# Modulation weights: four buffers instead of two, dots one call behind the transfer, another spread of the pieces

## The chip, the cores and the metric

The kernel runs on one core of a Trainium2 chip. The core has five engines with instruction streams of their own: TensorE (PE, matrix products; PEld is its weight load), VectorE (DVE), ScalarE (ACT), GpSimd (POOL) and SyncE (SP), which here issues the transfers from the chip's memory to the core's. Each engine works through its stream in order; semaphores hold an instruction until what it reads is there or what it overwrites is free. The metric is the device time of one execution in microseconds (us).

## The reference

The model has two layers and a width of 1024. Two groups of 256 tokens run through it: the latent tokens (`LAT`) and the context tokens (`CTX`). Each layer is a half FFN, a mixer (attention in layer 0, an mLSTM in layer 1) and a second half FFN; after layer 1's mixer only the latent tokens are needed. Shift, scale and gate of all of these, nine vectors per layer and group, come from a condition vector:

```python
mod_lat = split((silu(c)     @ ada_w[i] + ada_b[i])[:, None, :], 9)
mod_ctx = split((silu(c_ctx) @ ada_w[i] + ada_b[i])[None, None, :], 9)

def half_ffn(h, shift, scale, gate, w_in, w_out, g, b):
    xm = h * (1.0 + scale) + shift
    a, u = split(xm @ w_in, 2)                 # w_in: 1024 x 5632
    y = (silu(a) * u) @ w_out                  # w_out: 2816 x 1024
    return layer_norm(ALPHA * h + 0.5 * gate * y, g, b)
```

`ada_w` is 2 x 1024 x 9216 in float32. All is computed in float32 accuracy.

## The kernel before

Activations lie transposed in the core's memory: 8 tiles of 128 channels by 512 tokens (`h`, in the order listings t_66). A float32 product is made of three matmuls, high times high, high times low and low times high (`mm3`, line 238). For this each weight piece of 128 x 1024 float32 (512 KB, `raw`, the transfer at line 207) is split: ScalarE casts the high part (line 222) and VectorE subtracts it for the low part (line 227). Seven split pairs are kept, so the weights run ahead of PE.

A half FFN runs in two halves of eleven units. An "in" unit `j` multiplies two weight pieces into the gate and the up product; `ffn_g` then does the Silu on ScalarE (line 568), the product with the up part on VectorE (line 569), and splits it into `gh` (a cast, line 222) and `gl` (a subtraction, line 227). After the eleven "in" units come eight "out" units `d`, which each multiply all eleven products by a piece of `ffn_out` and add the result into `h` with the gate (line 692). Two tiles of the residual are also scaled after each "in" unit, by VectorE and ScalarE (lines 543 and 544, `residual`).

The modulation vectors are not computed by PE. `ada_w` comes in pieces of 128 output channels by 1024 (512 KB; `ada_load`, the transfer at line 331, on SP's queue with the other weights), and VectorE takes the dot of a piece with silu(c), and with silu(c_ctx) where that is needed (`ada_dot`, line 337): one instruction per vector. 56 pieces of layer 0 are taken beside the first half FFN, and 72 of layer 1 beside layer 0's second and layer 1's first half FFN. The last 32 pieces of layer 1 have one dot each, all others two. The function `side` makes a callback for each unit, `("in", j)` or `("out", half, d)`, which `ffn` calls after it has written that unit: `pop` in the first half FFN, and `some(n)` in the two others, with `n` from the table `DOTS`, a number of dots. `some` loads a piece and writes its dots behind the load until the number is reached. The buffers of the pieces lie in a pool (`cp`) with the two condition vectors, of which the Silu (line 306) is taken once for each pool; the pool is closed at `SUMSAT`, the fifth "out" unit of the first half (`d == 4`), where the operands of fast products (`fast_operands`, `fast_sums`) take its place, and a new one is opened for the rest.

What sets the order: a scheduler arranges the instructions of each engine, but those that are pinned, the dots, the residual's updates and others, stay in program order on their engine. In front of the norm of each next stage (lines 440 to 522) stands a chain of VectorE and ScalarE work: subtracting the mean (447), squares (454), their sums (464), the reciprocal root, the scaled result in two parts (520 to 522). The mLSTM behind layer 1's first FFN begins with constants (transfer at line 1152, casts at 1154 and 1155, a VectorE sum at 1156, memsets at 1161) and a convolution (1177 to 1181).

Of the kernel before, what the change touches and what calls it, by code (L numbers as in the profile page):

```python
# [18 lines left out]
P = 128  # L19
# [68 lines left out]

SUMSAT = 4
FLIP = 56  # L90
DOTS = {
    1: {("in",): 4, ("out", 0): 3, ("out", 1): 2},
    2: {("in",): 3, ("out", 0): 2, ("out", 1): 3},
}

TAILSTEP = {(0, 3, 1): 'bmccccccc', (1, 0, 2): 'c', (1, 0, 6): 'v', (1, 1, 7): 'rxxxxxxxx'}
# [73 lines left out]
class Body:  # L170
# [98 lines left out]
    def setup(self):  # L269
        nc, a = self.nc, self.a  # L270
        self.cols = col = self.t([P, 3 * BLOCK // 2])
        for i, x in enumerate((1.0, 1.0 / D, 1.0 / (D - P), 0.5 / D)):
            nc.vector.memset(col[:, i : i + 1], x)
        self.mean1, self.half = col[:, 1:2], col[:, 3:4]
        self.ones, self.mean, self.most = (col[:, i : i + 1].broadcast_to([P, P]) for i in range(3))

        self.h = self.t([P, ND, T])
        self.xh = self.t([P, ND, T + BLOCK], F32R)
        self.xl = self.t([P, ND, T + BLOCK], F32R)
        self.ident = self.t([P, P])  # L280
        self.vec = self.t([P, V_N])
        self.mod = {}
        self.s1 = {}

    def silu_c(self):

# [40 lines left out]
    def ada_load(self, layer, dt):  # L327
        if (layer, dt // ND) not in self.mod:
            self.mod[layer, dt // ND] = self.t([P, 2, ND])
        r = self.t([P, 1024], tag="ada", bufs=2, pool=self.cp)  # L330
        self.nc.sync.dma_start(r, self.a["ada_w"][layer, dt])
        return r

# [9 lines left out]
    def ada(self, layer, dt, vecs=(0, 1)):  # L343
        r = self.ada_load(layer, dt)
        for v in vecs:
            self.ada_dot(r, layer, dt, v)

    def modv(self):
        return self.t([P, 2, ND], tag="modv", bufs=12)
# [308 lines left out]
    def ffn(self, layer, s, gate, groups, side, start=None, cpool=None):  # L658
        nc, V = self.nc, self.nc.vector
        li = layer * 2 + s  # L660
        allg = BOTH
        call = lambda *k: side.get(k, lambda: None)()
        with self.tc.tile_pool(name=f"ffn{li}", bufs=1) as gp:
            self.gp, self.gt, self.gw, self.gn = gp, {}, T, NFH
            done = 0
            if start:
                start(self)
                done = NSTART

            def unit_in(j, w, g, steps={}, ks=range(ND), ps=None):  # L670
                n = g[1] - g[0]
                pa, pu = ps or (self.mm(), self.mm())
                for k in ks:
                    for part, o in ((0, pa), (1, pu)):
                        self.mm3(o[:, :n], w(part_k(part, k)), self.x(k, g), k == 0, k == ND - 1)
                    self.steps(steps.get((j, k), ""))
                if ks[-1] < ND - 1:
                    return pa, pu
                self.ffn_g(j, pa, pu, g)

            def unit_out(hf, d, w, g, steps={}):
                t0, t1 = g
                y = self.mm()
                for i in range(NFH):
                    gh, gl = self.gt[hf * NFH + i]
                    self.mm3(y[:, : t1 - t0], w(d * NFH + i), (gh[:, t0:t1], gl[:, t0:t1]), i == 0, i == NFH - 1)
                    self.steps(steps.get((int(g == CTX), d - (ND - TAIL), i), ""))
                for gg in groups:
                    if gg[0] >= t0 and gg[1] <= t1:
                        v = 0 if gg[0] == 0 else 1  # L690
                        z = self.h[:, d, gg[0] : gg[1]]
                        V.scalar_tensor_tensor(z, y[:, gg[0] - t0 : gg[1] - t0], gate()[:, v, d : d + 1], z, ALU.mult, ALU.add)  # L692
                        if hf:
                            self.add_sum(gg, d)

            w_in, w_out = self.a["ffn_in"][li], self.a["ffn_out"][li]
            stream = lambda j: Stream(self, [w_in[2 * j + i] for i in range(2)])
            for hf in range(2):
                js = list(range(hf * NFH, (hf + 1) * NFH))[0 if hf else done :]
                if hf == 0 and not start:  # L700
                    first = js[:LEAD]
                    ws = {j: Keep(self, [w_in[2 * j + i] for i in range(2)], SH) for j in first}
                    assert len(self.running) == 1

                    k0, k1 = range(ND // 2), range(ND // 2, ND)
                    for j in first[:-1]:
                        unit_in(j, ws[j], LAT, LEADSTEP[li])
                    j = first[-1]
                    ps = unit_in(j, ws[j], LAT, ks=k0)
                    assert not self.running  # L710
                    pc = unit_in(first[0], ws[first[0]], CTX, ks=k0)
                    ws[j](ND)
                    unit_in(first[0], ws[first[0]], CTX, ks=k1, ps=pc)
                    unit_in(j, ws[j], LAT, ks=k1, ps=ps)
                    for j in first[1:]:
                        unit_in(j, ws[j], CTX)
                    for j in first:
                        call("in", j)
                    js = js[LEAD:]
                fast = cpool is not None and hf == 1  # L720
                for j in js:
                    if fast:
                        self.fast_in(j, w_in, st)
                        continue
                    unit_in(j, stream(j), allg)
                    assert not self.running
                    if j >= LEAD + FAFTER:
                        self.fine = False
                    call("in", j)
                    self.residual(2, self.pin)  # L730
                if not hf:
                    self.residual(len(self.later))
                w = Stream(self, [w_out[hf * NFH + i] for i in range(NFH)])
                body = ND - TAIL if hf else ND
                if fast:
                    more.close()
                    cpool = self.silu_all()
                for d in range(body):
                    if cpool and not hf and d == SUMSAT:
                        cpool.close()  # L740
                        self.n += 1
                        more = ExitStack()
                        st = more.enter_context(self.tc.tile_pool(name=f"st{self.n}", bufs=1, side="right"))
                        self.fast_operands(st)
                    unit_out(hf, d, w, allg)
                    if cpool and not hf and d >= SUMSAT and d - SUMSAT < 2:
                        self.fast_sums(d - SUMSAT)
                    call("out", hf, d)
                if body < ND:
                    w = Keep(self, w.chunks, SH, w)  # L750
                    self.fine = True
                    for g in groups:
                        for d in range(body, ND):
                            unit_out(hf, d, w, g, TAILSTEP)
                    self.steps('B')
        return cpool
# [823 lines left out]
def emit(ctx, tc, a, out):  # L1580
    b = Body(ctx, tc, a, out)
# [16 lines left out]
    def side(key, coef, keep=(True, True), nxt=True, alone=False, dots={}):  # L1598
        def pop():
            for _ in range(3 if len(queue) > 40 else 2):  # L1600
                if queue:
                    b.ada(*queue.pop(0))

        def some(n):
            while n > 0 and later:
                n -= len(later[0][2])
                b.ada(*later.pop(0))

        get = once(key, coef)

        b.begin = lambda g: b.norm(g, get, keep[0 if g == LAT else 1], nxt, alone)
        s = {}
        for j in range(NF):
            s["in", j] = (lambda: some(dots["in",])) if dots else pop
        for d in range(ND):
            s["out", 0, d] = (lambda d=d: some(dots["out", 0] if d < SUMSAT else 0)) if dots else pop
            s["out", 1, d] = lambda: some(dots.get(("out", 1), 0))
        return s

    both = (LAT, CTX)  # L1620
# [5 lines left out]
    cpool = b.ffn(0, 1, once("g1", lambda: b.half_gate(0, 8)), both, side("n2", lambda: b.ln_mod(0, 2, (1, 0)), dots=DOTS[1]), cpool=cpool)  # L1626
    cpool = b.ffn(1, 0, once("g2", lambda: b.half_gate(1, 2)), both, side("n3", lambda: b.ln_mod(1, 0, (1, 3)), (True, False), dots=DOTS[2]), cpool=cpool)
    assert not later, len(later)
    cpool.close()
    b.mlstm(lambda: b.shift_(1, 5, slice(0, 1)), side("n4", lambda: b.ln_mod(1, 1, (1, 6), 1), alone=True))  # L1630
    b.ffn_last(1, once("g3", lambda: b.half_gate(1, 8, 1)))
# [93 lines left out]
```

## Time and profile before

| | |
|---|---|
| median of 3 runs | 1651.09 us (1650.75 to 1655.48) |
| the profiled execution | 1649.32 us, span 1647.6 us |
| mean granted TensorE clock | 0.993 |
| PE, PEld busy | 1617.8 us, 1457.4 us |
| VectorE busy | 1353.8 us |
| ScalarE busy | 744.2 us |
| GpSimd busy | 61.6 us |
| share of 16 transfer engines, main queue | 47.8% |

The profile is one execution. A row of the timeline gives start and length of a run of like instructions and, in brackets, how long the engine stood idle before it and for what; "t" stands for any unnamed tile. A row of the waits gives the sum, the number and the longest. A window's row gives the length, the busy time of each engine with its count, the granted clock, the share of the transfer engines and their rate. Layer 1's first half FFN has its "in" units from about 970 to 1043 us in this execution, the first "out" units behind them.

### The profile page before, as it was taken

The page shows a single profiled execution, that of the slowest core. Times are in us where ns is not written, and L with a number is a line of the kernel's source. Part 1 is how long each engine was busy: PE and PEld are TensorE (multiplying, and loading weights), DVE is VectorE, ACT ScalarE, POOL GpSimd, SP SyncE. Part 2 cuts the span into 40 slices and gives each one's busy share as a digit, 9 for nine tenths or more (in the row PEclk, how much of TensorE's full clock was granted, in tenths as well). Part 3 has the DMA queues.
Part 4 walks back from the last instruction along what each step waited for, and adds up shares of the span by engine and source line. Part 5 has one row for each costly group of instructions (what it writes and reads, how often), then busy time and mean ns, then how long its engine had stood idle before and what let it go on. Part 6 is the DMA issues. An engine that isn't in the chain of part 4 may idle for free. (4 is left out here: it accounts for less than half of the span.)

```text
span 1647.6 us, 26587 instructions
## 1 busy us (share of the span) xinstructions
PE 1617.8 (98%) x10308; PEld 1457.4 (88%) x10308; DVE 1353.8 (82%) x2689; ACT 744.2 (45%) x1269; POOL 61.6 (4%) x76
## 2 busy tenths in 40 slices
PE   9999999999999999999999999899999999999998
PEld 6888888899988998889999998689999989999987
DVE  5899978649888879999977977799965968897687
ACT  5532222314676343425652433225652656656542
POOL 0000000001011200000000100000000100020000
PEclk9999999999999999999999999899999999999999
DMA  9577765622103247733353267733352342437652
GB/s 371 187 237 231 239 215 187 203 76 84 65 1 91 64 143 229 229 128 129 103 182 126 78 193 255 250 120 116 115 155 66 116 120 78 135 109 256 181 172 96
DMA packets 72495, 252.59 MB, mean 153 GB/s; under 512 B 7984, under 2 KB 10800, under 8 KB 72368
## 3 DMA queue, kind: packets, MB, share of 16 engines
q1 hardware_dynamic: 71792, 250.10, 47.8%
q8 instruction: 81, 1.33, 0.3%
q10 hardware_dynamic: 576, 0.79, 0.1%
q14 instruction: 46, 0.38, 0.1%
HBM read 249.81 MB, written 1.05 MB: 152 GB/s over the span
## 5 line engine op out<-in xcount | busy, mean ns | idle before, releaser
L238 PE MATMUL t<-t,t 128*128 128x256 f32 (+2 forms) x8412 | 1325.1, 319 | 14.2 <-ACT t L222 10.7
L238 PEld LDWEIGHTS t<-t,t 128*128 128x128 f32 x8412 | 1193.1, 189 | 133.9 <-ACT t L222 12.7
L222 ACT CAST t<-t 128x1024 fp32r<-128x1024 f32 (+3 forms) x521 | 429.6, 844 | 467.3 <-PE t L238 244.3
L227 DVE TENSOR_TENSOR t<-t,t 128x256 fp32r<-128x256 f32 (+2 forms) x740 | 514.7, 728 | 116.6 <-ACT t L222 112.5
L337 DVE SCALAR_TENSOR_TENSOR t<-t,t 128x1024 bf16<-128x1024 f32 x224 | 263.5, 1220 | 25.2 <-DMA t<-in_ada_w 24.5
L909 PE MATMUL t<-t,t 128*128 128x256 f32 (+1 forms) x256 | 79.5, 311 | 0.0
L911 PE MATMUL t<-t,t 128*128 128x256 f32 (+1 forms) x256 | 78.8, 308 | 0.0
L910 PE MATMUL t<-t,t 128*128 128x256 f32 (+1 forms) x256 | 78.4, 306 | 0.0
L568 ACT ACTIVATE t<-t 128x512 f32<-128x512 f32 (+1 forms) x71 | 34.3, 487 | 95.6 <-PE t L238 95.6
L692 DVE SCALAR_TENSOR_TENSOR t<-t,t,t 128x256 f32<-128x256 f32 x96 | 42.7, 478 | 37.0 <-PE t L238 37.0
L569 DVE TENSOR_TENSOR t<-t,t 128x512 f32<-128x512 f32 (+1 forms) x71 | 38.9, 551 | 32.8 <-PE t L238 26.7
L464 POOL TENSOR_TENSOR t<-t,t 128x256 f32<-128x256 f32 x30 | 23.4, 781 | 1130.9 <-ACT t L454 1129.7
L1424 PE MATMUL t<-t,t 128*128 128x512 f32 (+3 forms) x286 | 60.2, 365 | 2.0 <-ACT t L1501 1.0
L837 PE MATMUL t<-t,t 128*128 128x512 f32 (+1 forms) x300 | 60.7, 364 | 0.0
L1424 PEld LDWEIGHTS t<-t,t 128*128 128x128 f32 (+2 forms) x286 | 43.8, 159 | 18.3 <-issue 2.2
L837 PEld LDWEIGHTS t<-t,t 128*128 128x128 f32 x300 | 51.4, 189 | 9.1 <-DVE t L831 0.3
L454 ACT ACTIVATE t<-t 128x256 f32<-128x256 f32 x72 | 26.2, 411 | 72.3 <-DVE t L447 72.3
L544 ACT ACTIVATE t<-t,t 128x256 f32<-128x256 f32 x64 | 29.4, 503 | 57.4 <-DVE t L543 57.4
L909 PEld LDWEIGHTS t<-t,t 128*128 128x128 f32 x256 | 48.4, 189 | 2.7
L910 PEld LDWEIGHTS t<-t,t 128*128 128x128 f32 x256 | 48.2, 188 | 2.6
L911 PEld LDWEIGHTS t<-t,t 128*128 128x128 f32 x256 | 48.1, 188 | 2.5
L615 DVE TENSOR_TENSOR t<-t,t 128x512 f32<-128x512 f32 x66 | 45.3, 686 | 1.1 <-DMA t<-in_ffn_in 0.3
(200 smaller groups left out, 1065.5 us busy)
## 6 DMA issues: line engine op xcount, KB each, us to landing
t<-in_ffn_in SPq DMA_DIRECT2D x168, 512.0 KB, 4.1
t<-in_ada_w SPq DMA_DIRECT2D x137, 512.0 KB, 4.2
t<-in_ffn_out SPq DMA_DIRECT2D x66, 512.0 KB, 4.4
t<-in_ffn_last SPq DMA_DIRECT2D x22, 512.0 KB, 3.5
t<-in_att_in SPq DMA_DIRECT2D x12, 512.0 KB, 3.5
t<-in_c SPq DMA_DIRECT2D x8, 512.0 KB, 7.8
t<-in_att_out SPq DMA_DIRECT2D x8, 512.0 KB, 3.5
t<-in_ml_qk SPq DMA_DIRECT2D x8, 512.0 KB, 3.6
```

The costliest lines, as they stand in the source:

```text
L222: self.behind(self.nc.scalar.copy(h, x))
L227: self.behind(self.nc.vector.tensor_tensor(out=ls, in0=xs, in1=hs.bitcast(F32), op=ALU.subtract))
L238: mm = lambda *k, **kw: self.nc.tensor.matmul(*k, skip_group_check=not group, **kw)
L337: ins = nc.vector.scalar_tensor_tensor(self.tmp().bitcast(BF16), r, 1.0, self.cb[:, v, :], ALU.mult, ALU.mult, accum_out=to)
L569: V.tensor_tensor(out=sl, in0=sl, in1=pu[:, :n], op=ALU.mult)
L615: add = lambda o, x, y: V.tensor_tensor(out=o, in0=x, in1=y, op=ALU.add)
L692: V.scalar_tensor_tensor(z, y[:, gg[0] - t0 : gg[1] - t0], gate()[:, v, d : d + 1], z, ALU.mult, ALU.add)
L837: pin(nc.tensor.matmul(o, gs[g], ws[k][w][:, i : i + n], start=k == k0 and g == w == 0, stop=k == k1 - 1 and g == 1,))
L909: mm(o, self.xh[:, k, c], wh, start=k == 0, stop=False)
L910: mm(o, self.xh[:, k, c], wl, start=False, stop=False)
L911: mm(o, self.xl[:, k, c], wh, start=False, stop=k == ND - 1)
L1424: mm = lambda *k, **kw: pin(nc.tensor.matmul(*k, **kw))
```

## The change

Three things change. The pieces get `PIECES = 4` buffers instead of two, in all three FFNs. In the second and third of them `some(n)` first writes the dots of the pieces that the call before has loaded (`flush`), and then loads `n` pieces whose dots are left to the next call; what is left is flushed before a pool is closed. The table `DOTS` now counts pieces, for each unit apart. In layer 0's second half FFN that is 2 pieces after each of the eleven "in" units as before, then 2, 2, 1, 1 (before: 2 each) and 1 each in the second half. In layer 1's first it is 2 pieces after the first four "in" units (before: 2 after three), 3 after the next five and 2 after the last two (before: 3 after all others), 2, 2, 2, 0 in the first four "out" units (before: 2 each), and 2, 2, 2, 1 in the first "out" units of the second half (before: none).

```diff
+PIECES = 4
 DOTS = {
-    1: {("in",): 4, ("out", 0): 3, ("out", 1): 2},
-    2: {("in",): 3, ("out", 0): 2, ("out", 1): 3},
+    1: {**{("in", j): 2 for j in range(11)}, **{("out", 0, d): 2 if d < 2 else 1 for d in range(4)}, **{("out", 1, d): 1 for d in range(4)}},
+    2: {**{("in", j): 2 for j in range(4)}, **{("in", j): 3 if j < 9 else 2 for j in range(4, 11)}, **{("out", 0, d): 2 if d < 3 else 0 for d in range(4)},
+        **{("out", 1, d): 2 if d < 3 else 1 for d in range(4)}},
 }
...
-        r = self.t([P, 1024], tag="ada", bufs=2, pool=self.cp)
+        r = self.t([P, 1024], tag="ada", bufs=PIECES, pool=self.cp)
...
+    def flush(self):
+
+        while self.waiting:
+            r, layer, dt, vecs = self.waiting.pop(0)
+            for v in vecs:
+                self.ada_dot(r, layer, dt, v)
...
                     if cpool and not hf and d == SUMSAT:
+                        self.flush()
                         cpool.close()
...
         def some(n):
-            while n > 0 and later:
-                n -= len(later[0][2])
-                b.ada(*later.pop(0))
+            b.flush()
+            for _ in range(min(n, len(later))):
+                layer, dt, vecs = later.pop(0)
+                b.waiting.append((b.ada_load(layer, dt), layer, dt, vecs))
...
-            s["in", j] = (lambda: some(dots["in",])) if dots else pop
+            s["in", j] = (lambda j=j: some(dots.get(("in", j), 0))) if dots else pop
         for d in range(ND):
-            s["out", 0, d] = (lambda d=d: some(dots["out", 0] if d < SUMSAT else 0)) if dots else pop
-            s["out", 1, d] = lambda: some(dots.get(("out", 1), 0))
+            s["out", 0, d] = (lambda d=d: some(dots.get(("out", 0, d), 0))) if dots else pop
+            s["out", 1, d] = lambda d=d: some(dots.get(("out", 1, d), 0))
...
     assert not later, len(later)
+    b.flush()
     cpool.close()
```

Lines of the changed kernel have numbers 2 to 11 higher (337 becomes 340, 207 becomes 209, 543 and 569 become 553 and 579). A row of the following listings is one instruction with what it writes and reads.

First place: VectorE in layer 1's first half FFN, at the last "in" unit (its product is t_10396 in the listing of before, and t_10376 in that of after; t_10318, t_10322 and t_10326 are pieces that the same call has loaded, t_10222, t_10224 and t_10226 pieces of the call before). Before:

```order
L337 SCALAR_TENSOR_TENSOR t_10320,t_10238<-t_10318,t_8504 128x1024
L337 SCALAR_TENSOR_TENSOR t_10324,t_10238<-t_10322,t_8504 128x1024
L227 TENSOR_TENSOR t_10651<-t_10649,t_10651 128x1024
L337 SCALAR_TENSOR_TENSOR t_10328,t_10238<-t_10326,t_8504 128x1024
L543 SCALAR_TENSOR_TENSOR t_66<-t_66,t_9031,t_9401 128x256 x2
L569 TENSOR_TENSOR t_10396<-t_10396,t_10335 128x512
L227 TENSOR_TENSOR t_10395<-t_10396,t_10394 128x512
L337 SCALAR_TENSOR_TENSOR t_10403,t_10238<-t_10401,t_8504 128x1024
L337 SCALAR_TENSOR_TENSOR t_10407,t_10238<-t_10405,t_8504 128x1024
```

After:

```order
L340 SCALAR_TENSOR_TENSOR t_10299,t_10059<-t_10222,t_8492 128x1024
L340 SCALAR_TENSOR_TENSOR t_10301,t_10059<-t_10224,t_8492 128x1024
L340 SCALAR_TENSOR_TENSOR t_10303,t_10059<-t_10226,t_8492 128x1024
L553 SCALAR_TENSOR_TENSOR t_66<-t_66,t_9014,t_9384 128x256 x2
L229 TENSOR_TENSOR t_10582<-t_10580,t_10582 128x1024
L579 TENSOR_TENSOR t_10376<-t_10376,t_10315 128x512
L229 TENSOR_TENSOR t_10623<-t_10621,t_10623 128x1024
L229 TENSOR_TENSOR t_10375<-t_10376,t_10374 128x512
L340 SCALAR_TENSOR_TENSOR t_10381,t_10059<-t_10305,t_8492 128x1024
L340 SCALAR_TENSOR_TENSOR t_10383,t_10307<-t_10308,t_8492 128x1024
```

Three dots stand ahead of the product in both; in the second the pieces they read were loaded a call earlier, and the subtraction of a weight piece that stood among them is behind the residual's updates.

Second place: SP's queue at the first "in" units of the same FFN. Before:

```order
L207 DMA t_10169<-in_ffn_in 128x1024
L207 DMA t_10198<-in_ffn_in 128x1024
L331 DMA t_9779<-in_ada_w 128x1024
L331 DMA t_9785<-in_ada_w 128x1024
L207 DMA t_10253<-in_ffn_in 128x1024
L331 DMA t_9791<-in_ada_w 128x1024
L331 DMA t_9797<-in_ada_w 128x1024
L207 DMA t_10282<-in_ffn_in 128x1024
L331 DMA t_9804<-in_ada_w 128x1024
L331 DMA t_9808<-in_ada_w 128x1024
```

After:

```order
L209 DMA t_10151<-in_ffn_in 128x1024
L209 DMA t_10180<-in_ffn_in 128x1024
L334 DMA t_9769<-in_ada_w 128x1024
L334 DMA t_9779<-in_ada_w 128x1024
L334 DMA t_9781<-in_ada_w 128x1024
L334 DMA t_9791<-in_ada_w 128x1024
L334 DMA t_9793<-in_ada_w 128x1024
L334 DMA t_9877<-in_ada_w 128x1024
L334 DMA t_9879<-in_ada_w 128x1024
L209 DMA t_10234<-in_ffn_in 128x1024
L334 DMA t_9881<-in_ada_w 128x1024
```

Where transfers of one weight piece and two pieces of `ada_w` took turns, seven pieces of `ada_w` now stand in a row.

Third place: VectorE between the end of that FFN and the context norm of the mLSTM (t_12243, then t_12215, is a sum over channels; t_66 is `h`). Before:

```order
L404 TENSOR_TENSOR t_12243<-t_12243,t_66 128x256
L1156 TENSOR_TENSOR t_12832<-t_69 128x64
L404 TENSOR_TENSOR t_12243<-t_12243,t_66 128x256
L1161 MEMSET t_12838 128x16 x2
L227 TENSOR_TENSOR t_12992<-t_12990,t_12992 128x256 x4
L1179 SCALAR_TENSOR_TENSOR t_12874<-t_12841,t_70,t_12874 128x255
L447 TENSOR_TENSOR t_66<-t_66,t_12891 128x256
L1180 SCALAR_TENSOR_TENSOR t_12874<-t_12841,t_70,t_12874 128x255
L447 TENSOR_TENSOR t_66<-t_66,t_12891 128x256 x3
```

After:

```order
L414 TENSOR_TENSOR t_12215<-t_12215,t_66 128x256
L229 TENSOR_TENSOR t_12992<-t_12990,t_12992 128x256
L414 TENSOR_TENSOR t_12215<-t_12215,t_66 128x256
L340 SCALAR_TENSOR_TENSOR t_12822,t_10555<-t_12374,t_12163 128x1024
L229 TENSOR_TENSOR t_12992<-t_12990,t_12992 128x256
L1167 TENSOR_TENSOR t_12832<-t_69 128x64
L1172 MEMSET t_12838 128x16 x2
L1190 SCALAR_TENSOR_TENSOR t_12874<-t_12841,t_70,t_12874 128x255
L457 TENSOR_TENSOR t_66<-t_66,t_12891 128x256
```

The last dot (line 340) stands behind the last sum, the mLSTM's first instructions behind it, and two of the four subtractions have moved further back.

More of the change, by code (lines that the diff above doesn't have):

```diff
@@ L283, in setup @@
         self.s1 = {}
+        self.waiting = []
     def silu_c(self):
```

## The prediction

> **What bounds the kernel now.** I read the page's busy shares first, then the list of waits, then timelines of one engine each around the longest wait. Durations come from one execution of 1649.32 us, whose span is 1647.6 us; the median of the runs shown, 1651.09 us, is 1.77 us above it. A change of 0.3% (5 us) is about what a measurement of this kernel can tell from none.
>
> ```profile
> span 1647.6 us, 26587 instructions
> ...
> PE 1617.8 (98%) x10308; PEld 1457.4 (88%) x10308; DVE 1353.8 (82%) x2689; ACT 744.2 (45%) x1269; POOL 61.6 (4%) x76
> ...
> L337 DVE SCALAR_TENSOR_TENSOR t<-t,t 128x1024 bf16<-128x1024 f32 x224 | 263.5, 1220 | 25.2 <-DMA t<-in_ada_w 24.5
> ```
>
> The columns of the last row are busy time, mean of one in ns, idle time before them and its cause. PE is busy 98% of the span, so a gain can only come out of the 30 us in which it is not, or out of a slower clock. The dots of the change (L337) cost VectorE 263.5 us, and in front of them it waits 24.5 us for their pieces. VectorE is busy 82%, so that matters only where PE then waits for VectorE. The list of PE's waits, and PE's timeline, show one such place:
>
> ```profile
> PE t L238 <- ACT t L222: 10.7, 4, 7.5
> PE t L1024 <- DVE t L227: 1.7, 2, 1.1
> ...
> 1029.65 20.11 PE L238 MATMUL t<-t,t 128*128 128x512 f32 x88
> 1057.31 22.97 PE L238 MATMUL t<-t,t 128*128 128x512 f32 x89 [7.55 <-ACT t L222]
> ```
>
> (The waits' columns are total, times, longest; the timeline's are start and length in us.) PE stands still for 7.55 us up to 1057.31, in the first half of layer 1's first FFN, where the "in" units have ended and the first "out" unit has begun; it waits for a cast. The next row's longest wait is 1.1 us. PE's windows around it (length, busy and count, granted clock, DMA share, GB/s) price the stall:
>
> ```profile
> 1040.00:1049.00 9.00, 9.00 (x42) 1.00 0.68 228
> 1049.00:1057.00 8.00, 0.76 (x4) 0.70 0.80 268
> 1057.00:1064.00 7.00, 6.69 (x18) 0.62 0.62 213
> 1064.00:1075.00 11.00, 11.00 (x50) 1.00 0.85 260
> ```
>
> From 1064 on, 50 matmuls take 11.00 us, 0.22 us each. The 22 of 1049 to 1064 would take 4.84 us and took 15.00: the stall costs 10.16 us, 2.6 us more than the gap, since the granted clock is 0.62 after it. This is 10.2 us of the whole, and the only sizeable one.
>
> Why the cast is late, backwards: ScalarE, VectorE and the DMA queue, word for word.
>
> ```profile
> 1047.71 0.59 ACT L568 ACTIVATE t<-t 128x512 f32<-128x512 f32 x1
> 1055.65 0.91 ACT L544 ACTIVATE t<-t,t 128x256 f32<-128x256 f32 x2 [7.36 <-DVE t L543]
> 1056.64 1.56 ACT L222 CAST t<-t 128x512 fp32r<-128x512 f32 x2
> ...
> 1049.25 1.22 DVE L337 SCALAR_TENSOR_TENSOR t<-t,t 128x1024 bf16<-128x1024 f32 x1
> ...
> 1050.40 1.22 DVE L227 TENSOR_TENSOR t<-t,t 128x1024 fp32r<-128x1024 f32 x1
> 1053.98 1.23 DVE L337 SCALAR_TENSOR_TENSOR t<-t,t 128x1024 bf16<-128x1024 f32 x1 [2.37 <-DMA t<-in_ada_w]
> ...
> 1055.13 0.88 DVE L543 SCALAR_TENSOR_TENSOR t<-t,t,t 128x256 f32<-128x256 f32 x2
> 1055.93 0.68 DVE L569 TENSOR_TENSOR t<-t,t 128x512 f32<-128x512 f32 x1
> ...
> 1049.36 1.47 SPq L331 DMA_DIRECT2D t<-in_ada_w  x2
> ```
>
> The cast at 1056.64 needs the product L569 of the last "in" unit. Its Silu (L568) was ready at 1048.30, but the product ran at 1055.93, behind three dots and two residual updates (L543). The third dot waited 2.37 us for a piece that could be requested only at 1049.36, when the dot before had freed one of two buffers. This has built up over the whole half: in the stretch of the "in" units, VectorE's waits are
>
> ```profile
> DVE t L337 <- DMA t<-in_ada_w: 14.9, 14, 2.8
> DVE t L227 <- ACT t L222: 6.1, 8, 1.1
> ```
>
> **The change, part by part.**
>
> *Four buffers, dots one call later.* The number of dots ahead of the last unit's product stays the same (I count 33 in both orders, from the first dot of this FFN), so VectorE's work up to there is unchanged. What can go is the 14.9 us of waiting. In the new order a unit of three pieces issues its second and third transfer when the first two dots of the call before have freed buffers, and needs them a call later. Between lies one unit's work on VectorE. The window of one unit length, and the time to landing of these transfers:
>
> ```profile
> 1004.00:1015.00 11.00, 11.00 (x50) 9.09 (x50) 7.95 (x16) 2.92 (x6) 0.00 (x0) 1.00 0.71 242
> ...
> DMA to landing us min/median/max: 3.4/4.2/5.6
> ```
>
> (PE, PEld, DVE, ACT, POOL busy.) VectorE is busy 7.95 us of 11, and a piece lands after 4.2, at worst 5.6 us. 7.95 − 5.6 leaves 2.3 us, so no dot waits, and per unit some 3 us of lag is worked off. Bounds: if all 14.9 us go, the product of the last unit runs as soon as its Silu is there. The product started 1055.93 − 1048.30 = 7.63 us after that Silu, and the Silu itself stood in ScalarE's queue behind residual updates that waited for VectorE as well. PE could go on without it until 1057.31 − 7.55 = 1049.76. So 7.6 us of the 14.9 are enough to close the gap, half of them. Lower bound: none of the waits go, gain 0. Upper bound: the stall is gone, gain 10.2 us. I take the upper end, because it has 7.3 us to spare.
>
> *Other spread of the pieces.* Two pieces instead of three or four dots' worth per unit at the head of this half, 33 pieces instead of 38 before its second half, and 7 instead of none in that second half: 7 × 1.22 = 8.5 us more there for VectorE, where PE doesn't wait for it now. In the FFN before, 32 pieces instead of 34. I cost these at 0; the cover is VectorE's idle time, 18% of the span. If it were gone there, the sums of the fast products would be late next.
>
> *The transfers on SP's queue.* Seven pieces now stand in a row ahead of one piece of in-weights (t_10253, in the new order t_10234), where two did:
>
> ```profile
> 971.82 2.62 SPq L331 DMA_DIRECT2D t<-in_ada_w  x2
> 975.25 0.33 SPq L207 DMA_DIRECT2D t<-in_ffn_in  x1
> ...
> L337 DVE SCALAR_TENSOR_TENSOR t<-t,t x35: 1215/1221/1228, 969.4 to 1059.0; 128x1024 bf16<-128x1024 f32 x35
> ...
> L207 SPq DMA_DIRECT2D t<-in_ffn_out x11: 327/328/328, 999.3 to 1062.2; - x11
> ```
>
> The last of the seven waits for the block of 14 dots, 14 × 1.15 = 16.1 us (1.15 is the distance of 1049.25 and 1050.40) from 969.4, the first dot here, so these weights are asked for at about 985.5 instead of 975.25, 10 us later. Weights run far ahead: the first of "out" is asked for at 999.3 and PE gets to "out" near 1043 (30 matmuls of 0.22 us before 1049.76), 44 us later, of which landing, cast and subtraction take their part. Bounds 0 and a stall of what exceeds that lead; I take 0.
>
> *SiLU of c for layer 1.* With 24 KB the buffer of c no longer fits beside the attention's, so its loads and two activations move from the first FFN's end to the attention's end, where ScalarE is idle:
>
> ```profile
> 323.75 1.06 ACT L306 ACTIVATE t<-t 128x1024 f32<-128x1024 f32 x1 [1.03 <-DMA t<-in_c]
> ...
> 547.77 1.41 ACT L454 ACTIVATE t<-t 128x256 f32<-128x256 f32 x4 [11.32 <-DVE t L447]
> ...
> 576.57 1.28 ACT L568 ACT_TABLE_LOAD   x1
> ...
> DMA to landing us min/median/max: 4.1/7.8/9.5
> ```
>
> Two activations of 1.06 us and a table load of 1.28 us (that of 576.57 moves here with them) are 3.4 us, in a gap of 11.32. Asked for when the gap begins, at 547.77 − 11.32 = 536.45, the buffer lands by these rows at 540.6 to 546, and the activations end at 544 to 549.4. Bounds: 0, and 1.6 us late at the norm whose squares start at 547.77. I take 0, the landing being nearer its minimum where the queue isn't full.
>
> *The last flush.* One dot, 1.15 us, now stands on VectorE between the end of "out" and the context norm of the mLSTM, and tiles of the mLSTM share the memory that closes after it:
>
> ```profile
> 1284.95 0.28 ACT L1155 CAST t<-t 128x128 fp32r<-128x128 f32 x1
> 1285.14 0.40 ACT L1154 CAST t<-t 128x256 fp32r<-128x256 f32 x1
> 1287.09 0.56 ACT L1177 ACTIVATE t<-t,t 128x256 f32<-128x256 f32 x1 [1.55 <-PE t L238]
> 1289.68 0.42 ACT L454 ACTIVATE t<-t 128x256 f32<-128x256 f32 x1 [2.02 <-DVE t L447]
> ...
> 1282.04 0.33 SPq L1152 DMA_DIRECT2D t<-in_const  x1
> ...
> 1287.78 1.09 DVE L227 TENSOR_TENSOR t<-t,t 128x256 fp32r<-128x256 f32 x3
> ...
> 1295.75 1.05 PE L427 MATMUL t<-t,t 128*128 128x1 f32 x8 [0.69 <-DVE t L464]
> ```
>
> PE waits 0.69 us for this norm, so a delay here shows in full. The dot adds 1.15 us; four subtractions (1.09 / 3 = 0.36 each) leave the stretch up to the norm's last sum, 1.45: −0.3 us. The two casts at 1284.95 now wait for the dot, about 3 us, and would still end before the 1289.68 square. If the constants' transfer also waited for the dot (near 1288, 6 us later; it now takes up to 1284.95 − 1282.04 = 2.9 us), the casts would come near 1291 and 1291.5 and hold up the square by about 2 us, with what follows up to 3. Bounds −0.3 and +3; I take 0, since the order lets that transfer go after a norm step that stands ahead of the dot.
>
> *Sum.* 1649.32 − 10.2 + 0 = 1639.1 us for a profiled execution, and 1651.09 − 10.2 = **1640.9 us** as a median: 0.6% faster.
>
> **The rivals.**
>
> *Partly handed back.* The stall goes, but the last flush or the moved SiLU costs 2 to 4 us at its norm. For it: PE's 0.69 us wait there shows no slack. Against it: the working above. 1641 + 3 = 1644 us.
>
> *The stall only shrinks.* VectorE keeps half of its waits or new ones behind ScalarE (the 6.1 us row). With a gap of 3 us left, priced by the stall's own ratio 10.16 / 7.55 = 1.35, 4 us stay: 1645 us; with nothing gained, as the change then does nothing where PE waits, 1651 us. Against it: twice the waiting that must go can go. The Trainium skill (TensorE: Matmul & The Clock Gate, section on the HAM clock gate) says that the clock halves after an idle window of about 3.4 us and comes back after a busy one. The fall to 0.62 after 7.55 us agrees; no row here shows a gap near 3 us. By that rule a 3 us gap would leave the clock alone and cost 3.0, so 1644 us.
>
> *Slower: weights behind waiting pieces.* SP issues in order; a piece that waits for its buffer, which a lagging VectorE frees, holds all weights behind it. The point from which it decides: the weights' lead of 44 us less landing, cast and subtraction (about 15 us), some 29 us. If the pieces were held four more units of 11 us, 44 us, PE would stand 15 us, at 1.35 that is 20: 1651 − 10 + 20 = 1661 us. For it: seven pieces in a row, four buffers that VectorE frees one by one. Against it: I find 10 us of delay, not 29. The Trainium skill (DMA: Bandwidth & Descriptors, Anatomy of one DMA) says that a semaphore wait sits on the issuing sequencer ahead of dispatch, which speaks for this rival; the rows of two pieces in 2.62 and 1.47 us, where one issue takes 0.33, agree.
>
> **How the numbers follow.** Stall gone and little else: 0.60, 1638.5 to 1643. Partly handed back: 0.17, 1643 to 1647. Only shrunk, or unchanged: 0.14, 1644 to 1652. Slower by the weights: 0.09. The predicted time is that of the first, 1641. The range takes in the first two and most of the third: 1637.5 to 1649. Faster by more than 0.3% (below 1646.1): 0.60 + 0.15 + 0.05 = 0.80; within 0.3%: 0.02 + 0.08 + 0.01 = 0.11; slower: 0.09.
>
> **What would show it.** Right: no PE gap above 1.5 us between 1000 and 1100, granted clock 1.00 there, VectorE's waits for pieces down from 24.5 us to under 5, and the last "in" unit's product within 3 us of its Silu. The SiLU of c in ScalarE's gap near 540, with PE's waits up to 580 as short as now; PE's waits from 1275 to 1310 under 3 us in sum. Wrong: a PE gap behind the cast of a product still there, PE waiting for a weight's cast or subtraction in any FFN, or a gap before the norms named. I would be most wrong if VectorE's lag came from the order of the work and not from the waits for pieces.

## The result, and the profile after

| | before | after |
|---|---|---|
| median | 1650.92 us (4 runs, 1649.79 to 1655.48) | 1638.72 us (4 runs, 1638.02 to 1640.61) |
| profiled execution | 1649.32 us, span 1647.6 us | 1640.61 us, span 1638.8 us |
| mean granted clock | 0.993 | 0.999 |

The ratio is 0.9925, with a 95% interval of 0.9907 to 0.9943: the kernel is 0.75% faster, 12.2 us. The forecast was 1641 us with a range of 1637.5 to 1649. A second set of five executions gave 1639.39 us against 1651.36 us, ratio 0.9922 (0.9910 to 0.9934); of the eleven executions of before in it, one of 2002.23 us at a mean granted clock of 0.752 is left out. The profile of before is of an execution 1.6 us under its median, that of after of one 1.9 us above its own.

The page after, the rows that answer to those of before:

```profile
span 1638.8 us, 26592 instructions
...
PE 1616.8 (99%) x10308; PEld 1455.5 (89%) x10308; DVE 1353.5 (83%) x2689; ACT 745.4 (45%) x1269; POOL 62.0 (4%) x76
...
L340 DVE SCALAR_TENSOR_TENSOR t<-t,t 128x1024 bf16<-128x1024 f32 x224 | 260.7, 1219 | 0.0
```

VectorE's 224 dots take what they took, but the idle time in front of them fell from 25.2 us to 0.0. PE's busy time is 1 us less; the span is 8.8 us shorter. PE's waits for the cast fell from 10.7 us (longest 7.5) to 3.1 (longest 1.8). At the turn from "in" to "out" in layer 1's first half FFN, PE's timeline and windows (length, busy and count, granted clock, transfer share, GB/s):

```profile
999.79 110.38 PE L240 MATMUL t<-t,t 128*128 128x512 f32 x518
```

```profile
1040.00:1049.00 9.00, 9.00 (x42) 1.00 0.64 210
1049.00:1057.00 8.00, 8.00 (x37) 1.00 0.93 307
1057.00:1064.00 7.00, 7.00 (x33) 1.00 0.71 216
1064.00:1075.00 11.00, 11.00 (x50) 1.00 0.31 109
```

One run of 518 matmuls without a gap, and 70 matmuls in the 15 us from 1049 to 1064 where 22 stood before, at full clock. VectorE and ScalarE at the last "in" unit:

```profile
1038.79 1.22 DVE L229 TENSOR_TENSOR t<-t,t 128x1024 fp32r<-128x1024 f32 x1
1042.68 0.69 DVE L579 TENSOR_TENSOR t<-t,t 128x512 f32<-128x512 f32 x1 [2.67 <-ACT t L578]
```

```profile
1041.99 0.60 ACT L578 ACTIVATE t<-t 128x512 f32<-128x512 f32 x1 [2.57 <-PE t L240]
1042.61 1.57 ACT L224 CAST t<-t 128x1024 fp32r<-128x1024 f32 x2
```

Before, the product (line 569, now 579) came 7.6 us after its Silu, behind three dots. Now VectorE stands idle for 2.67 us until the Silu is there, and the Silu itself waits for PE and not for VectorE.

Between two marks that both kernels have, PE's first norm matmul of the context group at 910.12 (909.77 after) and the same at 1275.66 (1265.00), the time went from 365.54 to 355.23 us: 10.3 us less in the stretch that holds the stall. The rest of the profiled executions differs by 1.5 us in sum and in both directions: 1.1 us later at the start, 1.5 us earlier through the attention, 0.2 us earlier at the start of the mLSTM, 2.0 us later behind it.

### The profile page after: what moved, and what is told of

Same layout as the page of the kernel before. It is cut to its first block, busy times and chain, and to the rows that moved or that the text cites. A ratio compares the mean times of both kernels' runs of the same rounds, so it can differ in the third digit from the quotient of the medians.

```text
span 1638.8 us, 26592 instructions
## 1 busy us (share of the span) xinstructions
PE 1616.8 (99%) x10308; PEld 1455.5 (89%) x10308; DVE 1353.5 (83%) x2689; ACT 745.4 (45%) x1269; POOL 62.0 (4%) x76
## 5 line engine op out<-in xcount | busy, mean ns | idle before, releaser
L531 ACT ACTIVATE t<-t,t 128x256 fp32r<-128x256 f32 x72 | 32.8, 503 | 27.4 <-DVE t L530 27.4
```

## The experiments

"Gap" is PE's idle time at the turn from "in" to "out" in layer 1's first half FFN. "Marks" is the time between the two norm matmuls named above.

| run | ratio to before (95%) | median us | gap us | marks us |
|---|---|---|---|---|
| after, again | 0.9922 (0.9910 to 0.9934) | 1639.39 | 0 | 355.13 |
| four buffers alone | 0.9928 (0.9916 to 0.9940) | 1640.25 | 0 | 356.77 |
| dots a call behind, three buffers | 0.9931 (0.9918 to 0.9944) | 1640.17 | 0 | 355.23 |
| new spread alone | 0.9960 (0.9948 to 0.9973) | 1645.10 | 3.23 + 0.84 | 362.92 |
| after, 6 dots more at the end | one run | 1637.39 | 0 | 355.62 |
| after, 8 dots more at the end | 0.9931 (0.9907 to 0.9956) | 1639.43 | 0 | 355.90 |
| after, 14 dots more at the end | 0.9956 (0.9944 to 0.9967) | 1644.17 | 0.26 | 361.53 |
| after, 14 dots more at the head | 1.0006 (0.9994 to 1.0018) | 1651.37 | 0 | 368.01 |
| after, "out" in program order | 0.9920 (0.9899 to 0.9942) | 1638.13 | 0 | 355.17 |
| the same, 8 dots more | 0.9962 (0.9948 to 0.9976) | 1644.96 | 2.97 + 0.52 | 362.08 |
| the same, 14 dots more | 1.0016 (1.0006 to 1.0025) | 1653.71 | 11.59 | 369.92 |
| after, no dot ahead of the mLSTM's norm | 0.9920 (0.9903 to 0.9938) | 1638.37 | 0 | 355.37 |

### Again

> The changed kernel once more, for its own spread and for a second profile. If the gain is the stall of 10.2 us and the chance of a run, 0.6 to 0.75% below the kernel before, 1639 to 1641 us; the 2 us that the first profile lost behind 1400 us and the 1.1 us that it lost before 15 us are then not there again. If those are the change's doing, they stand in this profile too.

1639.39 us, and again 10.4 us less between the marks. The 1.1 us at the start were 0.4 this time; the 2 us behind 1300 us came again (341.6 us from 1297.02 to the end, where before had 339.2). Measured from the second mark to the end, the fourteen profiles lie between 371.7 and 375.4 us (before 371.9, after 373.8, again 374.1), in no order that goes with their edits. So most of it is the spread of this stretch; that a part of it is the change's doing stays open, with one profile of before.

### The three parts, one at a time

Four buffers and nothing else:

```diff
-        r = self.t([P, 1024], tag="ada", bufs=2, pool=self.cp)
+        r = self.t([P, 1024], tag="ada", bufs=4, pool=self.cp)
```

> The kernel before with four buffers for the pieces and nothing else. If the waits for buffers were the cause, VectorE's waits for pieces fall from 24.5 us to under 6, the gap of PE at 1049.76 goes and the time is 1640 to 1642 us. If the dots must stand a call behind their transfers, the third piece of a call still comes too late: over 12 us of waits stay, a gap of 3 to 7 us, 1644 to 1650 us.

The dots one call behind, with three buffers and the spread of before:

```diff
-PIECES = 4
+PIECES = 3
 DOTS = {
...
+    1: {**{("in", j): 2 for j in range(11)}, **{("out", 0, d): 2 if d < 4 else 0 for d in range(4)}, **{("out", 1, d): 1 for d in range(4)}},
+    2: {**{("in", j): 2 if j < 3 else 3 for j in range(11)}, **{("out", 0, d): 2 for d in range(4)}},
```

> The dots one call behind the transfers with three buffers, the fewest with which it can be done, and the spread of before. If time between transfer and dot is what counts, no gap and 1640 to 1642 us. If the number of buffers is, a third of the waiting stays: a gap of 1 to 4 us and 1643 to 1647 us.

The new spread, with two buffers and each dot behind its load:

```diff
-PIECES = 4
+PIECES = 2
...
-            b.flush()
             for _ in range(min(n, len(later))):
-                layer, dt, vecs = later.pop(0)
-                b.waiting.append((b.ada_load(layer, dt), layer, dt, vecs))
+                b.ada(*later.pop(0))
```

> The new spread of the pieces alone, two buffers and dots at once. By the waits theory VectorE still waits 12 us or more for pieces in the in units, and the gap stays, shorter by the one piece that the last call no longer has: 4 to 7 us, 1645 to 1650 us. If the spread is what freed VectorE at the end, no gap and 1639 to 1641 us.

The waits for pieces on VectorE in the run with the dots behind, and in that with the spread alone, followed by PE's timeline and windows in the latter:

```profile
DVE t L339 <- DMA t<-in_ada_w: 0.2, 1, 0.2
```

```profile
DVE t L340 <- DMA t<-in_ada_w: 24.9, 31, 3.0
...
1039.72 14.44 PE L240 MATMUL t<-t,t 128*128 128x512 f32 x63
1057.39 0.50 PE L240 MATMUL t<-t,t 128*128 128x512 f32 x1 [3.23 <-ACT t L224]
1058.73 16.50 PE L240 MATMUL t<-t,t 128*128 128x512 f32 x65 [0.84 <-DVE t L229]
...
1049.00:1057.00 8.00, 5.16 (x23) 1.00 0.60 204
1057.00:1064.00 7.00, 5.77 (x18) 0.76 0.85 271
```

Four buffers alone take the waits away (no row of waits for these dots is left) and the gap with them; so do three buffers with the dots a call behind. Their intervals and that of all three parts together overlap, so nothing more is gained by having both that these runs can tell. What the two have in common is that a transfer is asked for earlier before its dot; in the kernel before these transfers took 3.4 to 5.6 us to land. Three buffers with each dot behind its load were not run, so what the third buffer does without the later place of the dots stays open. The new spread alone leaves 24.9 us of waits, as before, and still halves the gap; the call after the tenth "in" unit loads two pieces instead of three, which is the likely reason. (Its profile is of an execution of 1649.38 us, 4 us above its median; 2.2 us of that are in the first 380 us.) With either of the others it adds nothing that these runs can tell.

Between the marks the kernel with four buffers alone took 1.5 us longer than the changed one, without a gap at the turn. That is a loss of clock elsewhere, behind a wait of 1.03 us at the context norm near 929 (0.60 before, 0.58 after):

```profile
930.78:934.19 3.41, 3.41 (x19) 0.50 0.78 241
```

At half the clock, 3.41 us of work lose 1.7. The run with the spread alone has such a stretch there too, the twelve other profiles none. That the edits have to do with it is not shown.

### How much VectorE may lag at the turn

The last dot ahead of the last unit's product is repeated (for 6, 8 and 14):

```diff
+EXTRA, WHERE = 6, (1, 54)
...
             for v in vecs:
-                self.ada_dot(r, layer, dt, v)
+                for _ in range(1 + (EXTRA if (layer, dt) == WHERE else 0)):
+                    self.ada_dot(r, layer, dt, v)
```

> The changed kernel with the last dot ahead of the last in unit's product taken six times more (same input, same place of the sum; only time is added). In the profile of the changed kernel VectorE waited 2.67 us for that unit's Silu, its product began at 1042.68, and PE needs the cast 1.4 us after it begins; PE would have come to the cast's product near 1049.4, so 2.67 + 5.35 = 8.0 us of more work are free. Six dots and one subtraction that moves ahead of it are 8.0 us: no gap of PE, at most 0.8 us. If the stall of before was due to transfers and not to VectorE's lag, nothing here makes one either, and the next two stay without a gap as well.

> The same with eight more: 9.2 us and one subtraction of 1.1, 10.3 us, so a gap of 2.3 us. At the stall's ratio of 1.35 that costs 3.1 us, with the clock unharmed 2.3 us; the 3.23 us gap of the run with the spread alone was followed by a lower clock, so a part of a clock loss is likely.

> The same with fourteen more: 16.1 us and two subtractions, 18.4 us, so a gap of 10.4 us and, with the clock behind it, 13 us: 1652 to 1653 us.

Six dots: no gap, as expected. Eight: no gap either, where 2.3 us were expected, and 1639.43 us. Fourteen: the product began at 1059.43, 1.0 us later than 18.4 us more of work put it, but PE hardly stood still, and the kernel lost 5 us, not 13:

```profile
1060.81 19.39 PE L241 MATMUL t<-t,t 128*128 128x512 f32 x84 [0.26 <-ACT t L225]
...
1095.20 5.07 PE L241 MATMUL t<-t,t 128*128 128x512 f32 x14 [2.07 <-DVE t L230]
```

The expectation had left out that PE's order is arranged anew for each kernel. In the order of the kernels before and after, PE takes all 33 matmuls of the first "out" unit, then all of the second. With 14 dots more it takes 30 of the first, 30 of the second and 20 of the third, and only then the last product of the first: the late product was known and was moved. With eight, 13 matmuls of the second unit (2.9 us) stand ahead of that product, with six 5 of them (1.1 us), so neither of these runs tests the room of 8.0 us. What is left with 14 is a later wait, for a subtraction among VectorE's work for the fast products, 2.07 us at 1095.20 with slow matmuls behind it (5.07 us for 14).

So the same was run with the first three "out" units held to program order:

```diff
-                    self.mm3(y[:, : t1 - t0], w(d * NFH + i), (gh[:, t0:t1], gl[:, t0:t1]), i == 0, i == NFH - 1)
+                    self.mm3(y[:, : t1 - t0], w(d * NFH + i), (gh[:, t0:t1], gl[:, t0:t1]), i == 0, i == NFH - 1, pin=li == 2 and not hf and d < 3)
```

> The changed kernel with the first three out units of that half FFN held to program order on PE (each of their products finished before the next begins). That is the order it has anyway: 1638 to 1641 us, no gap at the turn.

> The same with the eight dots more. VectorE's product then begins near 1050.95 as in the run with eight dots and free order, and PE can go on 1.4 us later, at 1052.3, instead of 1049.4: a gap of 2.9 us. By the ratio 1.35 of the first stall 3.9 us in all, 1643 us; with the clock unharmed 2.9 us, 1642 us. If the product of the last unit does not stand on PE's path, no gap.

> The same with the fourteen dots more. The product begins near 1059.4, PE goes on near 1060.8 instead of 1049.4: a gap of 11.4 us, with the clock behind it 13 to 15 us. The 5 us that the run in free order lost near 1095 are then hidden, since what is late there is late behind the gap: 1652 to 1655 us.

PE in the runs with 8 and with 14, timeline and windows:

```profile
1052.53 0.57 PE L241 MATMUL t<-t,t 128*128 128x512 f32 x1 [2.97 <-ACT t L225]
1053.62 56.63 PE L241 MATMUL t<-t,t 128*128 128x512 f32 x239 [0.52 <-DVE t L230]
...
1049.00:1057.00 8.00, 4.51 (x12) 0.74 0.54 146
1057.00:1064.00 7.00, 7.00 (x26) 0.81 0.79 284
```

```profile
1060.04 50.23 PE L241 MATMUL t<-t,t 128*128 128x512 f32 x208 [11.59 <-ACT t L225]
...
1040.00:1049.00 9.00, 8.45 (x38) 1.00 0.39 119
1049.00:1057.00 8.00, 0.00 (x0) 0.68 0.21 66
1057.00:1064.00 7.00, 3.96 (x9) 0.50 0.39 101
1064.00:1075.00 11.00, 11.00 (x47) 0.93 0.67 227
```

2.97 us where 2.9 were expected, 11.59 where 11.4 were: the lag of VectorE at the turn, less 8 us, is PE's gap. The time came back too: with 14 dots the kernel is as slow as before and a little slower. The price of a short gap was wrong. Eight dots cost 6.8 us (1644.96 against 1638.13, the latter of two executions), not 3 to 4; this is taken up in the last section.

### Lag at the head instead

```diff
+EXTRA, WHERE = 7, (1, 36)
```

> Fourteen more dots (seven for each vector) as in the run before, but at the head of the same FFN, at the third in unit's first piece. VectorE works off about 3 us of lag in each of the seven to eight units after it, 21 to 24 us, more than the 16.1 us: no gap at the turn to out, within 1 us of the changed kernel. If weights behind waiting pieces are as near as the slower rival feared, they come 16 us later than in the changed kernel, 26 us later than before, and PE waits for a cast or subtraction of a weight between 1000 and 1040.

```profile
1003.47 1.65 PE L241 MATMUL t<-t,t 128*128 128x512 f32 x3 [4.52 <-ACT t L580]
1009.53 70.73 PE L241 MATMUL t<-t,t 128*128 128x512 f32 x300 [4.42 <-DVE t L581]
...
990.00:1020.00 30.00, 21.06 (x78) 0.77 0.44 127
```

Of the expectation only the turn came true. There is no gap there, and the last unit's product waited for its Silu again (1.69 us), so the lag was worked off on the way. But PE stood twice before, for 8.9 us, the clock fell behind it, and the kernel lost all of its gain instead of staying within 1 us. PE did not wait for weights, as the other side had it: the releasers are a Silu and a product of the "in" units. In the kernel an "in" unit writes into two of the six accumulators of `mm`, so PE can begin a fourth unit only when the first one's are read. In this run that limit bound before the weights did.

### The dot ahead of the mLSTM

```diff
-        **{("out", 1, d): 2 if d < 3 else 1 for d in range(4)}},
+        **{("out", 1, d): n for d, n in enumerate((3, 2, 2))}},
```

> The changed kernel with the last four callbacks of pieces at 3, 2, 2 and 0 instead of 2, 2, 2 and 1, so that no dot stands behind the last out unit and in front of the mLSTM's context norm. If that dot costs what it lasts, 1.2 us less from 1265 to 1300; by the prediction's sum, which let four subtractions leave for the one dot, within 0.5 us of the changed kernel there, and the time the same.

PE's wait at that norm, without that dot and with it:

```profile
1285.82 1.05 PE L437 MATMUL t<-t,t 128*128 128x1 f32 x8 [0.59 <-DVE t L474]
```

```profile
1284.84 1.05 PE L437 MATMUL t<-t,t 128*128 128x1 f32 x8 [0.24 <-DVE t L474]
```

From the norm's matmul before (1265.57 and 1265.00) this one comes 20.25 us later without the dot and 19.84 with it. The dot costs nothing that shows there: from the last sums of "out" (line 414) to the norm's last sum (line 474), VectorE takes eight subtractions of 0.36 us without it and five with it, so what takes its place lasts about as long.

## Why the prediction was right

**What bounds the kernel.** The one gap of 7.55 us and the slow clock behind it were priced at 10.16 us; between the marks 10.3 us went. The chain (cast, product, dot, piece, buffer) holds: with buffers alone, which change neither the dots nor their order with the updates of the residual, the gap is gone.

**Half of the waits would do.** The sum took the upper end because 7.6 of 14.9 us were enough. All went, and the room is 8.0 us in the trace after; the runs in program order with 8 and 14 dots bear this out within 0.2 us.

**The other spread.** It was costed at 0. The kernel with the dots a call behind and the spread of before took 1640.17 us, the changed one 1638.72 and 1639.39; the intervals overlap, so the runs tell no cost and no gain.

**The transfers on SP's queue.** The forecast was a weight transfer at about 985.5 instead of 975.25:

```profile
971.42 14.08 SPq L334 DMA_DIRECT2D t<-in_ada_w  x7
986.94 0.33 SPq L209 DMA_DIRECT2D t<-in_ffn_in  x1
```

It was 986.94, and PE had no gap behind it. The slower rival, weights behind waiting pieces, did not come. With 16 us more of lag at the head another limit came first and held PE, so how much more the weights' lead would bear is not shown.

**SiLU of c.** It was forecast to end between 544 and 549.4, in a gap of 11.32 us:

```profile
538.44 1.28 ACT L309 ACT_TABLE_LOAD   x1 [2.01 <-DMA t<-in_c]
539.73 2.01 ACT L309 ACTIVATE t<-t 128x1024 f32<-128x1024 f32 x2
547.47 1.41 ACT L464 ACTIVATE t<-t 128x256 f32<-128x256 f32 x4 [5.72 <-DVE t L457]
```

It ended at 541.74, sooner than either bound, and 5.72 us of the gap are left.

**The last flush.** Its bounds were -0.3 and +3 us, taken as 0. The constants' transfer did not wait for the dot, the casts did, and both ended ahead of the squares:

```profile
1278.21 0.30 ACT L1166 CAST t<-t 128x128 fp32r<-128x128 f32 x1 [0.81 <-DVE t L340]
1278.42 0.40 ACT L1165 CAST t<-t 128x256 fp32r<-128x256 f32 x1
1279.52 0.42 ACT L464 ACTIVATE t<-t 128x256 f32<-128x256 f32 x1 [0.70 <-DVE t L457]
...
1272.17 0.33 SPq L1163 DMA_DIRECT2D t<-in_const  x1
```

PE's wait at that norm went from 0.69 to 0.24 us.

**Where it was off.** The gain was 12.2 us, and 12.0 in the second set, where 10.2 were forecast. No term of the sum accounts for this, and its cause stays open. The stretches outside the marks vary by more than that from one profile to the next: the first mark is reached between 908.05 and 912.90 us, and the stretch behind the second takes 371.7 to 375.4 us. A part of that is the clock, below. The step that was wrong is the ratio 10.16 / 7.55 = 1.35, by which the second rival priced a smaller gap: 4 us for 3 us of gap, where 3.5 us of gap cost 6.6 in the windows and 4.1 us cost 6.0. Had the gap only shrunk to 3 us, some 5 to 6 us of the stall would have stayed: 1646 to 1647 us, not 1645. The likeliest case did not hang on it.

## What to carry to other kernels

When a busy engine feeds the bounding one, read its waits as lag: here 14.9 us of waiting in 14 places added up silently, and showed as one gap where PE first needed the last unit, far from the transfers that caused them. Count what lag the consumer allows at that place, and remove at least the waiting beyond it; here two more buffers, or one more with the dots a call later, were enough, and everything beyond that brought nothing that could be measured. A lag can also be limited by something nearer than the queue one fears, here the accumulators, and a scheduler that knows of the lag may reorder around it.

## What the runs showed of the hardware that was not expected

What a gap of PE costs beyond itself does not follow its length. At 0.22 us for a matmul, from the windows shown:

| run | gap us | time lost, worked out | lost beyond the gap |
|---|---|---|---|
| before | 7.55 | 15.00 - 22 x 0.22 = 10.2 | 2.6 |
| new spread alone | 3.23 + 0.84 | 15.00 - 41 x 0.22 = 6.0 | 1.9 |
| in order, 8 dots more | 2.97 + 0.52 | 15.00 - 38 x 0.22 = 6.6 | 3.2 |
| in order, 14 dots more | 11.59 | 35.00 - 94 x 0.22 = 14.3 | 2.7 |
| 14 dots more at the head | 4.52 + 4.42 | 30.00 - 78 x 0.22 = 12.8 | 3.9 |

So 3.5 us of gap cost nearly twice their length, 11.6 us a quarter more. Windows cut where the granted clock changes show why. The first two rows are of the kernel before, the next two of the run in order with eight dots more; from 1062.38 and from 1059.65 on the clock is 1.00 again:

```profile
1048.73:1052.14 3.41, 1.03 (x5) 1.00 0.79 246
1052.14:1062.38 10.24, 5.07 (x11) 0.50 0.65 227
...
1049.41:1052.82 3.41, 0.44 (x2) 1.00 0.33 94
1052.82:1059.65 6.83, 6.31 (x15) 0.50 0.81 256
```

The clock is 1.00 or 0.50, and it is 0.50 for one, two, three or four times 3.41 us (in the five runs of the table 10.24, 3.41, 6.83, 13.65 and 13.65 us). What PE works in that time goes at half speed: 5.07 us lose 2.5, and 6.31 lose 3.2, which is about what the table counts. A gap that ends early in such a stretch costs more behind it than one that fills it.

The rule weighed in the prediction (the Trainium skill, TensorE: Matmul & The Clock Gate, section on the HAM clock gate), that idle time up to a window of about 3.4 us leaves the clock alone, did not hold as it was used there: in the run with eight dots more the clock fell at 1052.82, after 2.97 us of idle time and 0.29 us of work, and ahead of the gap of 0.52 us.

Even less can do it. In the attention PE waits 0.68 and 1.16 us, 0.4 us of work apart. Before, and after:

```profile
459.94 0.38 PE L238 MATMUL t<-t,t 128*128 128x256 f32 x1 [0.68 <-ACT t L222]
461.49 3.04 PE L238 MATMUL t<-t,t 128*128 128x256 f32 x12 [1.16 <-DVE t L227]
...
458.22:461.63 3.41, 1.57 (x12) 1.00 0.01 2
461.63:465.04 3.41, 3.41 (x17) 0.50 0.00 0
```

```profile
460.69 0.39 PE L240 MATMUL t<-t,t 128*128 128x256 f32 x1 [0.68 <-ACT t L224]
462.23 1.81 PE L240 MATMUL t<-t,t 128*128 128x256 f32 x12 [1.16 <-DVE t L229]
...
457.62:461.03 3.41, 2.73 (x19) 1.00 0.01 2
461.03:464.45 3.42, 2.26 (x18) 1.00 0.00 0
```

The same 12 matmuls took 3.04 us in the one and 1.81 us in the other. Of the 14 profiles 8 show a clock of 0.50 for 3.41 us at this place.

Three falls of the clock in the kernel before, at 461.63, 1052.14 and 1458.32, lie 173 and 119 times 3.4133 us apart, so they keep to one grid. In the 3.41 us of that grid that end at 461.63, both waits lie together, and PE works 1.57 us. In the profile after, the clock's only fall, at 1635.22 where the kernel's work ends, puts the grid at 461.03 (344 steps earlier): there the boundary lies between the two waits, PE works 2.73 and 2.26 us, and the clock stays. That fits a clock window that runs on by itself and is met at one place or another, as the Trainium skill has it on the same page; where the grid lies differs between these profiles, and in none was it set on purpose. How busy PE is does not decide alone: the fall at 1458.32 came after 3.12 us of work in 3.41. What does decide there is not shown.
